# Pairs 9 to 14 of an expert loop: transposes, lists and scale rows moved behind the gate-up products, and the order of the last sums

## Chip, cores and metric

One core of one Trainium2 chip. The metric is device time in microseconds (us) of one execution; lower is better.

## What is computed

A decoder layer for 512 tokens of width 1024: an input projection, two token mixers (dilated attention and a spatial gating unit), an output projection, a first layer norm, a mixture of 32 experts and a second layer norm. The change touches only the experts and the second norm. Cut to them, the reference is:

```
gate = g_onehot[:, :, None] * e_gate[:, None, :] * p_sel[:, None, None]   # top 1 of 4 groups, top 2 of 8 experts
for g in range(N_GROUPS):
    gu = einsum('td,edf->tef', t, w_gate_up[g]);  a, b = gu[..., :256], gu[..., 256:]
    act = silu(a) * b * gate[:, g, :, None]
    y = y + einsum('tef,efd->td', act, w_down[g])
h = layer_norm(alpha * h + y, ln2_g, ln2_b)
```

## The kernel before

All 32 experts' weights (3 MB each) are streamed from HBM. Experts go in 16 pairs, p = 0 to 15 (`LAST` is 15): an expert takes up to 64 tokens, so that a pair fills 128 rows. Weights come in pieces of 1 MB, six to a pair (four of gate-up, two of down), into 20 slots in SBUF (`wc`). `wfill` puts their DMAs on the queue of the sync engine (SP), in the order of use, each as soon as its slot has been read.

One pair is:

- **Gate-up** (`gate_up`, line 900): for k = 0 to 7 the two experts' products, each over one eighth of the width, summed in one PSUM tile. Steps 0 to 3 need the first two pieces, steps 4 to 7 the other two.
- **Gating** (`gated`, lines 1080 and 1081): ScalarE (ACT) takes the silu, VectorE (DVE) multiplies, into `sa`.
- **Transposing `sa`** (`act_transposed`, lines 1088 and 1090): two transposes on TensorE (PE), a copy by ACT into `aT`.
- **Down** (`down`, line 1105): the products with the down weights; ACT copies the sums out as `y` (line 1107), DVE takes each row's mean off (1113, 1114), and GpSimd (POOL) scatters the rows to `y_dram` by an indirect DMA (1115).

Beside it, work for later pairs: `transposed` (1075, 1076) turns the next pair's gathered rows `xg` into `xTm`, in two halves of four transposes each, the first half copied by DVE, the second by ACT. `fetch(p + 3)` makes the list of tokens of the pair three further on: eight small products (873), three small DVE operations (884, 889, 879) and the gather of the rows, an indirect DMA of POOL (892). `pair_sel` (868) prepares the selection matrix for it on DVE.

PE, DVE, ACT, POOL and SP run this stage in the order in which the code issues it. In pairs 1 to 8 the down step of a pair stands inside the next pair's gate-up. From pair 9 on (`ATONCE`) it follows its own gate-up at once, so that PE stands still until `sa` and then `aT` are there. In all pairs but the last, the transposes stand between the gate-up steps k = 4, 5 and 6, and `fetch` behind k = 5.

In pair 13 (`LAST - 2`), behind k = 6, eight products (1190) spread the scale and the shift of the second norm, held in 8 rows, over 128 partitions; ACT copies the sums (1192) into the slot `ln2`, four copies of 512 columns.

**The end.** All but the last pair's rows come back from `y_dram`: eight loads (1203) bring `rb`, two summands for each of the four tiles of 128 tokens; SP issues them when the last scatter has landed. The final sum of tile i, half n, is made in PSUM (`fin[i, n]`) from three parts: `fin_x` (1151) adds the centred input of the layer, `fin_y` (1222) the last pair's rows by products with a one-hot matrix `G`, and `fin_rows` (1228, 1229) the sum of the two `rb` rows, which DVE forms for tile 0 and POOL for the others, and which PE then adds to both halves. `mb` (1260) gives the means, `nx` (1261, 1262). Then for each tile ACT squares (1236), DVE scales (1241) and writes the output (1248), and SP stores it (1249).

Before, the order on PE is: `fin_x(2, 0)`, `fin_x(2, 1)` ahead of pair 15; behind its gate-up `fin_x(0, 0)`, the transposes of `sa`, `fin_x(1, 0)`, down, `fin_y` of tiles 0 to 2 first half, `fin_x(0, 1)`, `fin_x(1, 1)`, `fin_x(3, 0)`, `mb`, `fin_y` of tiles 0 to 2 second half, both halves of tile 3, and at last `fin_rows` of all four tiles. The PSUM tiles are a ring of four (`acc`) and two rings of two (`tp`, `sc`).

Of the kernel before, what the change touches and what calls it, by code (L numbers as in the profile page):

```python
# [16 lines left out]
ALU = mybir.AluOpType  # L17
# [8 lines left out]
NT = 4  # L26
# [5 lines left out]
LAST = NPAIR - 1  # L32

ATONCE = 9
# [24 lines left out]
def layer(tc, I, out):  # L59
    nc = tc.nc  # L60
    pe, dve, act, pool_e, sp = nc.tensor, nc.vector, nc.scalar, nc.gpsimd, nc.sync
# [10 lines left out]
    def open_pool(name, side="left", space=None):  # L72
        es = ExitStack()
        kw = dict(name=name, bufs=1, side=side)
        if space != DRAM:
            kw["reuse_waits"] = "tile"
        if space is not None:
            kw["space"] = space
        p = es.enter_context(tc.tile_pool(**kw))
        stacks[name] = es  # L80
        return p
# [16 lines left out]
    def ps_acc():  # L98
        return ps_pj.tile([128, 512], F32, name="acc", bufs=4)

    def ps_t():
        return ps_tp.tile([128, 4, 128], F32, name="tp", bufs=2)

    def ps_s():
        return ps_sc.tile([128, 512], F32, name="sc", bufs=2)
# [8 lines left out]
    zeros = const.tile([128, 256], F32, name="zeros")  # L114
    x_sb = const.tile([128, NT, D], F32, name="x_sb")
    ident = const.tile([128, 128], F32, name="ident")
# [404 lines left out]
    def wfill(n):  # L521

        for src in srcs[len(wq):n]:
            t = slots[len(wq) % NSLOT]()
            if isinstance(t, list):
                for z in range(2):
                    sp.dma_start(out=t[z], in_=src[:, z * D:z * D + D])
            else:
                sp.dma_start(out=t, in_=src)
                t = [t[:, z * D:z * D + D] for z in range(2)]  # L530
            wq.append(t)
# [124 lines left out]
    op = open_pool("op")  # L656
# [214 lines left out]
    def pair_list(p, ip, a, b):  # L871
        for z in range(8):
            pe.matmul(ip[:, a:b], sels[p][:, z], vals[:, z // 2, z % 2, a:b], start=(z == 0), stop=(z == 7))
# [117 lines left out]
    xgs = [xg12[:, p] for p in range(2)]  # L991
# [71 lines left out]
    xTm = [wk.tile([128, 2, 4, 128], F32, name="xTm", bufs=2) for _ in range(2)]  # L1063
# [7 lines left out]
    def transposed(xg, xT, kk):  # L1071
        xv = xg.rearrange("s (q k) -> s k q", k=KD)
        tp = ps_t()
        for j in range(4):
            pe.transpose(out=tp[:, j], in_=xv[:, kk * 4 + j], identity=ident)  # L1075
        (act.copy if kk else dve.tensor_copy)(xT[:, kk], tp)  # L1076
# [7 lines left out]
    def act_transposed(sa):  # L1084
        av = sa.rearrange("s (q c) -> s c q", c=2)
        tp = ps_s().rearrange("p (c s) -> p c s", c=4)
        for c in range(2):
            pe.transpose(out=tp[:, c], in_=av[:, c], identity=ident)
        aT = mo.tile([128, 2, 128], F32, name="aT", bufs=1)
        act.copy(aT, tp[:, 0:2])  # L1090
        return aT

    def down(p, aT, dp=None):

        dp = dp or [ps_acc() for _ in range(2)]
        y = [wk.tile([128, D], F32R, name="y", bufs=2) for _ in range(2 if p == LAST else 1)]
        y0 = y[0].bitcast(F32)
        rs = mo.tile([128, 4], F32, name="rs", bufs=2)
        for n in range(2):
            ns = slice(n * 512, n * 512 + 512)  # L1100
            for c in range(2):
                for z in range(2):
                    zs = slice(64 * z, 64 * z + 64)
                    w = wq[6 * p + 4 + z]
                    pe.matmul(dp[n][zs], aT[:, c, zs], w[c][:, ns], start=(c == 0), stop=(c == 1))  # L1105
            if p < LAST:
                act.activation(y0[:, ns], dp[n], AF.Copy, accum_out=rs[:, n:n + 1])  # L1107
            else:
                act.activation(y[0][:, ns], dp[n], AF.Copy, accum_out=rs[:, 2 * n:2 * n + 1])
                dve.scalar_tensor_tensor(y[1][:, ns], dp[n], 1.0, y0[:, ns], op0=ALU.mult, op1=ALU.subtract,  # L1110
                                         accum_out=rs[:, 2 * n + 1:2 * n + 2])
        if p < LAST:
            dve.tensor_scalar(rs[:, 2:3], rs[:, 0:1], rs[:, 1:2], -1.0 / D, op0=ALU.add, op1=ALU.mult)  # L1113
            dve.tensor_scalar(y0, y0, rs[:, 2:3], None, op0=ALU.add)
            pool_e.indirect_dma_start(out=y_dram[:, :], out_offset=bass.IndirectOffsetOnAxis(ap=tos[p][:, 0:1], axis=0),  # L1115
                                      in_=y0, in_offset=None, bounds_check=2 * S - 1, oob_is_err=False)
        wfill(6 * p + 6 + NSLOT)
        return y, rs
# [9 lines left out]
    def fetch(p):  # L1128
        if p < NPAIR:
            ip = ps_s()  # L1130
            pair_list(p, ip, 0, 7)
            pair_tok(p, ip, 2)
            pair_out(p, ip)
            gather(p)
# [7 lines left out]
    fin = {}  # L1142
    hs = [slice(0, 512), slice(512, D)]

    def fin_x(i, n):

        if (i, n) not in fin:
            fin[i, n] = (ps_acc, ps_s, ps_t, ps_acc)[i]()
            if i == 2:
                fin[i, n] = fin[i, n].rearrange("p a b -> p (a b)")  # L1150
        pe.matmul(fin[i, n], ident, x_sb[:, i, hs[n]], start=True, stop=False)

    for p in range(1, NPAIR):
        gp = ps_acc()
        if p == 3:

            for z, n in enumerate(("ln2_g", "ln2_b")):
                pool_e.dma_start(out=zeros[4 * z:4 * z + 4], in_=I[n].rearrange("o (a d) -> (o a) d", a=4))
        if p == LAST - 2:
            ln2 = slots[16]().rearrange("p (a d) -> p a d", a=2)  # L1160
            ln2_g, ln2_b = ln2[:, 0], ln2[:, 1]
        if p == LAST:
            for n in range(2):
                fin_x(2, n)
        for k in range(KD):
            gate_up(p, [xTm[p % 2][:, kk] for kk in range(2)], k, gp)
            if k == 0:
                pair_sel(p + 3, 0, NT)
            if k == 1 and p <= ATONCE:
                aT = act_transposed(sa)  # L1170
            if k == 3:
                if p <= ATONCE:
                    down(p - 1, aT)
                wfill(6 * p + 2 + NSLOT)
            if k == 6 and LAST - 2 - NT <= p < LAST - 2:

                i = p - LAST + 2 + NT
                t = st2[:, i]
                dve.tensor_reduce(t[:, 5:6], x_sb[:, i], axis=AX.X, op=ALU.add)
                dve.tensor_scalar(t[:, 5:6], t[:, 5:6], -1.0 / D, None, op0=ALU.mult)  # L1180
                dve.tensor_scalar(x_sb[:, i], x_sb[:, i], t[:, 5:6], None, op0=ALU.add)
            if k in (4, 5) and p < LAST:
                transposed(xgs[(p + 1) % 2], xTm[(p + 1) % 2], k - 4)
            if k == 5:
                fetch(p + 3)
            if k == 6 and p == LAST - 2:
                for j in range(4):
                    b = ps_s()
                    for z in range(2):
                        pe.matmul(b[:, 256 * z:256 * z + 256], ident[0:8, 2 * j + z:2 * j + z + 1].to_broadcast([8, 128]), zeros[0:8],  # L1190
                                  start=True, stop=True)
                    act.copy(ln2[:, j // 2, hs[j % 2]], b)
        wfill(6 * p + 4 + NSLOT)
        sa = gated(gp, tgs[p][:, 1:2])
        if ATONCE <= p < LAST:
            down(p, act_transposed(sa))

    rb = []
# [8 lines left out]
    fin_x(0, 0)  # L1207
    aT = act_transposed(sa)
    fin_x(1, 0)


    o2 = [slots[z]().rearrange("p (a d) -> p a d", a=2) for z in (1, 2)]
# [7 lines left out]
    def fin_y(i, n):  # L1220
        for z in range(2):
            pe.matmul(fin[i, n], G[:, i * 128:i * 128 + 128], y[z][:, hs[n]], start=False, stop=False)

    def fin_rows(i):

        for n in range(2):
            r = rb[i][0][:, hs[n]]
            (pool_e if i else dve).tensor_tensor(r, r, rb[i][1][:, hs[n]], op=ALU.add)
            pe.matmul(fin[i, n], ident, r, start=False, stop=True)

    def ln2_scale(i):
# [19 lines left out]
    y, rs = down(LAST, aT, dp)  # L1251
    for i in range(NT - 1):
        fin_y(i, 0)
    fin_x(0, 1)
    fin_x(1, 1)
    fin_x(NT - 1, 0)

    mb = fin[NT - 1, 1] = ps_acc()
    for i in range(NT):
        pe.matmul(mb[:, 4 * i:4 * i + 4], G[:, i * 128:i * 128 + 128].bitcast(F32), rs, start=True, stop=True)  # L1260
# [1 line left out]
    dve.tensor_scalar(nx, nx, -1.0 / D, None, op0=ALU.mult)  # L1262
    for i in range(NT - 1):
        fin_y(i, 1)
    fin_y(NT - 1, 0)
    fin_x(NT - 1, 1)
    fin_y(NT - 1, 1)
    for i in range(NT):
        fin_rows(i)
    for i in range(NT):  # L1270
        ln2_scale(i)
        ln2_out(i)
# [7 lines left out]
    with tc.If(full > CAP):  # L1280
# [4 lines left out]
        with tc.For_i(0, NE, 1) as e:  # L1285
# [13 lines left out]
            for i in range(NT):  # L1299
# [6 lines left out]
                for k in range(KD):  # L1306
                    pe.matmul(gp, xT[k // 4][:, k % 4], og[k // 4][:, (k % 4) * 512:(k % 4) * 512 + 512],
                              start=(k == 0), stop=(k == KD - 1))
                aT = act_transposed(gated(gp, og_t[:, i:i + 1]))
                dp = [ps_acc() for _ in range(2)]  # L1310
                for n in range(2):
                    for c in range(2):
                        pe.matmul(dp[n], aT[:, c], od[:, c * 1024 + n * 512:c * 1024 + n * 512 + 512],
                                  start=(c == 0), stop=(c == 1))
# [38 lines left out]
```

## Time and profile before

| | us |
|---|---|
| median of 3 runs | 508.66 (508.55 to 509.71) |
| the profiled execution | 509.01 |
| its span in the profile | 507.3 |
| PE busy | 470.5 |
| DVE busy | 233.4 |
| ACT busy | 162.0 |
| POOL busy | 126.9 |

Times in the rows are counted from the start of the span. A busy time is an average over stages with different limits, so the stages around the change have to be read by themselves. A matmul record's duration is longer than the step to the next one, since they overlap; steps are read from starts, or from the chain of waits, which has them without overlap. The granted clock is given as a share of 2.4 GHz: 1.00 is 2.4 GHz and 0.50 is 1.2 GHz.

### The profile page before, as it was taken

To read this page: it belongs to the slowest core of one execution; us is meant where nothing else is said; L and a number is where in the kernel's file an instruction comes from. 1 tells how busy PE (TensorE), PEld (TensorE's weight loads), DVE (VectorE), ACT (ScalarE), POOL (GpSimd) and SP (SyncE) were. 2 spreads that over 40 slices of the span, in tenths; PEclk is the share of its full clock that TensorE was granted. 3 is DMA by queue.
4 is the path that set the end of the run, shared out by engine and by line. 5 is a ranking of instruction groups with operands and counts; after the bars stand their busy time and mean duration, and the time that the engine had idled before them with its cause. 6 is when DMAs were issued, how large, how long until landed. Compare 5 with 4: busy or idle time off the path is not lost.

```text
span 507.3 us, 6634 instructions
## 1 busy us (share of the span) xinstructions
PE 470.5 (93%) x2322; PEld 280.4 (55%) x2322; DVE 233.4 (46%) x600; ACT 162.0 (32%) x366; POOL 126.9 (25%) x194
## 2 busy tenths in 40 slices
PE   6999999999889999979999999999987988888991
PEld 5788887888767678859643333333332323323350
DVE  3586637723577548897522222222234233011056
ACT  4533536241578533123112222222221112212233
POOL 4025344000287710443111211111111010000350
PEclk9999999999999999998899999999999889979996
DMA  8744231740398549585599999999999999995624
GB/s 266 273 125 110 68 115 41 244 172 0 83 419 236 188 162 384 182 330 192 170 346 357 423 420 420 415 424 421 419 418 424 425 420 419 420 429 249 267 91 167
DMA packets 40805, 141.18 MB, mean 278 GB/s; under 512 B 10508, under 2 KB 14656, under 8 KB 28993
## 3 DMA queue, kind: packets, MB, share of 16 engines
q1 hardware_dynamic: 35808, 130.71, 67.3%
q0 software_dynamic: 4960, 10.01, 5.5%
q8 instruction: 20, 0.33, 0.3%
q14 instruction: 17, 0.13, 0.1%
HBM read 131.78 MB, written 16.25 MB: 292 GB/s over the span
## 4 chain that ended last, share of the span: by engine, by line
PE 57%; DMA 32%; DVE 7%; SPq 1%; ACT 1%; issue 1%; DVEq 0%; ACTq 0%
DMA wc<-in_w_gate_up 20%; PE acc L900 9%; PE acc L320 7%; PE acc L322 7%; PE acc L321 7%; PE acc L1105 5%; DMA wc<-in_w_down 4%; DMA wc19b<-in_w_gate_up 4%; PE acc L915 3%; DMA x_sb<-in_x 2%; PE acc L600 2%; PE tp L615 1%; PE acc L575 1%; PE acc L577 1%; PE acc L576 1%; PE tp L1075 1%
## 5 line engine op out<-in xcount | busy, mean ns | idle before, releaser
L900 PE MATMUL acc<-wc,xTm 128*64 128x512 f32 x456 | 118.0, 601 | 2.9 <-DMA wc<-in_w_gate_up 2.6
L320 PE MATMUL acc<-w_hi,xTh 128*128 128x512 f32 x160 | 65.2, 407 | 1.5 <-ACT w_hi L311 0.7
L1105 PE MATMUL acc<-wc,aT 128*64 128x512 f32 x248 | 63.7, 645 | 3.1 <-ACT aT L1090 3.1
L321 PE MATMUL acc<-w_lo,xTh 128*128 128x512 f32 x160 | 62.9, 393 | 0.5 <-DVE w_lo L312 0.5
L322 PE MATMUL acc<-w_hi,xTl 128*128 128x512 f32 x160 | 62.9, 393 | 0.0
L900 PEld LDWEIGHTS acc<-wc,xTm 128*64 128x64 f32 x456 | 31.6, 136 | 56.0 <-issue 45.3
L1115 POOL DMA_INDIRECT y_dram<-y,to x15 | 15.7, 1050 | 156.3 <-DVE xTm L1076 84.7
L1113 DVE TENSOR_SCALAR rs<-rs 128x1 f32<-128x1 f32 x15 | 3.2, 215 | 95.2 <-ACT y L1107 95.2
L312 DVE TENSOR_TENSOR w_lo<-w_raw,w_hi 128x512 fp32r<-128x512 f32 x40 | 28.1, 706 | 35.4 <-ACT w_hi L311 35.1
L311 ACT ACTIVATE w_hi<-w_raw 128x512 fp32r<-128x512 f32 x40 | 25.3, 631 | 54.2 <-PE acc L322 47.9
L1105 PEld LDWEIGHTS acc<-wc,aT 128*64 128x64 f32 x248 | 19.1, 148 | 42.1 <-issue 36.9
L1107 ACT ACTIVATE y<-acc 128x512 f32<-128x512 f32 x30 | 17.9, 597 | 61.9 <-PE acc L1105 61.9
L422 POOL TENSOR_TENSOR P<-P,st 128x128 f32<-128x128 f32 (+3 forms) x32 | 23.2, 748 | 51.1 <-DVE st L421 49.5
L320 PEld LDWEIGHTS acc<-w_hi,xTh 128*128 128x128 f32 x160 | 30.3, 189 | 8.6 <-ACT w_hi L311 1.4
L321 PEld LDWEIGHTS acc<-w_lo,xTh 128*128 128x128 f32 x160 | 30.3, 189 | 6.7 <-DVE w_lo L312 1.1
L322 PEld LDWEIGHTS acc<-w_hi,xTl 128*128 128x128 f32 x160 | 30.1, 188 | 6.7 <-DVE xTl L163 0.3
L1076 ACT COPY xTm<-tp 128x512 f32<-128x512 f32 x15 | 8.8, 585 | 63.8 <-PE tp L1075 63.8
L1075 PEld LDWEIGHTS tp<-ident,xg 128*128 128x128 f32 x120 | 15.5, 194 | 23.5 <-issue 15.4
L892 POOL DMA_INDIRECT xg<-h_dram,ti x15 | 15.8, 1050 | 43.9 <-issue 22.6
L1081 DVE SCALAR_TENSOR_TENSOR sa<-sa,tg,acc 128x256 f32<-128x256 f32 x16 | 7.6, 476 | 34.0 <-ACT sa L1080 34.0
L868 DVE TENSOR_TENSOR sel<-iota_v,slotp 128x1024 bf16<-128x1024 f32 (+2 forms) x23 | 22.5, 990 | 0.1
L1075 PE MATMUL tp<-ident,xg 128*128 128x128 f32 x120 | 21.0, 299 | 0.0
(330 smaller groups left out, 773.2 us busy)
## 6 DMA issues: line engine op xcount, KB each, us to landing
wc<-in_w_gate_up SPq DMA_DIRECT2D x61, 1024.0 KB, 20.1
wc<-in_w_down SPq DMA_DIRECT2D x31, 1024.0 KB, 20.7
w_raw<-in_w_in SPq DMA_DIRECT2D x18, 512.0 KB, 3.8
y_dram<-zeros SPq DMA_DIRECT2D x8, 512.0 KB, 7.8
wo_raw<-in_w_out SPq DMA_DIRECT2D x16, 256.0 KB, 3.6
wc<-y_dram SPq DMA_DIRECT2D x6, 512.0 KB, 7.5
x_sb<-in_x SPq DMA_DIRECT2D x8, 256.0 KB, 10.1
h_dram<-x_sb SPq DMA_DIRECT2D x4, 512.0 KB, 2.9
```

Of the source, the lines that this page charges most:

```text
L311: act.activation(wh, raw, AF.Copy)
L312: dve.tensor_tensor(wl, raw, wh.bitcast(F32), op=ALU.subtract)
L320: pe.matmul(acc[i], xh, wh, start=(k == 0), stop=False)
L321: pe.matmul(acc[i], xh, wl, start=False, stop=False)
L322: pe.matmul(acc[i], xl, wh, start=False, stop=(k == KD - 1))
L422: pool_e.tensor_tensor(P[:, 0:n], P[:, 0:n], bc(st4[:, 2:3], [128, n]), op=ALU.mult)
L868: dve.tensor_tensor(sels[p][:, 2 * a:2 * b], bc(iota_v.rearrange("p a b -> p (a b)")[:, None, :], [128, n, 128]), bc(slotp[:, p, a:b].rear ...
L892: pool_e.indirect_dma_start(out=xgs[p % 2], out_offset=None, in_=h_dram[:, :], in_offset=bass.IndirectOffsetOnAxis(ap=tis[p][:, 0:1], axis=0),
L900: pe.matmul(gp[zs], xT[k // 4][:, k % 4, zs], w[k % 4 // 2][:, k % 2 * 512:k % 2 * 512 + 512], start=(k == 0), stop=(k == KD - 1))
L1075: pe.transpose(out=tp[:, j], in_=xv[:, kk * 4 + j], identity=ident)
L1105: pe.matmul(dp[n][zs], aT[:, c, zs], w[c][:, ns], start=(c == 0), stop=(c == 1))
L1107: act.activation(y0[:, ns], dp[n], AF.Copy, accum_out=rs[:, n:n + 1])
```

## The change

For pairs 9 to 14 the two halves of `transposed` and `fetch(p + 3)` no longer stand between the gate-up steps. They follow `gated`, ahead of `act_transposed` and `down`. The eight products of the scale rows, all in pair 13 before, go to the same place: four of them, with two copies, in pair 13, and four in pair 14. At the end, `fin_x(0, 1)` and `fin_x(1, 1)` go ahead of the last down step. The sum of the two `rb` rows goes to POOL for tile 0 too. Each tile's `fin_rows` follows its `fin_y`, and all of tile 3 comes last.

```diff
-            if k in (4, 5) and p < LAST:
+            if k in (4, 5) and p < ATONCE:
                 transposed(xgs[(p + 1) % 2], xTm[(p + 1) % 2], k - 4)
-            if k == 5:
+            if k == 5 and p < ATONCE:
                 fetch(p + 3)
-            if k == 6 and p == LAST - 2:
-                for j in range(4):
-                    b = ps_s()
-                    for z in range(2):
-                        pe.matmul(b[:, 256 * z:256 * z + 256], ident[0:8, 2 * j + z:2 * j + z + 1].to_broadcast([8, 128]), zeros[0:8],
-                                  start=True, stop=True)
-                    act.copy(ln2[:, j // 2, hs[j % 2]], b)
         wfill(6 * p + 4 + NSLOT)
         sa = gated(gp, tgs[p][:, 1:2])
         if ATONCE <= p < LAST:
+            for kk in range(2):
+                transposed(xgs[(p + 1) % 2], xTm[(p + 1) % 2], kk)
+            fetch(p + 3)
+            if p >= LAST - 2:
+                a = p - LAST + 2
+                for j in range(2):
+                    b = ps_s()
+                    for z in range(2):
+                        r = 4 * a + 2 * j + z
+                        pe.matmul(b[:, 256 * z:256 * z + 256], ident[0:8, r:r + 1].to_broadcast([8, 128]), zeros[0:8],
+                                  start=True, stop=True)
+                    act.copy(ln2[:, a, hs[j]], b)
             down(p, act_transposed(sa))
...
     fin_x(1, 0)
+    fin_x(0, 1)
+    fin_x(1, 1)
...
-            (pool_e if i else dve).tensor_tensor(r, r, rb[i][1][:, hs[n]], op=ALU.add)
+            pool_e.tensor_tensor(r, r, rb[i][1][:, hs[n]], op=ALU.add)
...
     for i in range(NT - 1):
         fin_y(i, 0)
-    fin_x(0, 1)
-    fin_x(1, 1)
-    fin_x(NT - 1, 0)
-
+    fin[NT - 1, 0] = ps_acc()
     mb = fin[NT - 1, 1] = ps_acc()
...
     for i in range(NT - 1):
         fin_y(i, 1)
-    fin_y(NT - 1, 0)
-    fin_x(NT - 1, 1)
-    fin_y(NT - 1, 1)
-    for i in range(NT):
         fin_rows(i)
+    for n in range(2):
+        fin_x(NT - 1, n)
+        fin_y(NT - 1, n)
+    fin_rows(NT - 1)
     for i in range(NT):
         ln2_scale(i)
         ln2_out(i)
```

## Rows read from the trace of the kernel before

**Rows 1.** The head of the page, and of its 40 slices of the span the granted clock and the DMA share, both in tenths.

```profile
PE 470.5 (93%) x2322; PEld 280.4 (55%) x2322; DVE 233.4 (46%) x600; ACT 162.0 (32%) x366; POOL 126.9 (25%) x194
...
PEclk9999999999999999998899999999999889979996
DMA  8744231740398549585599999999999999995624
```

**Rows 2.** The chain of waits in order of time, 366 to 482 us: start, duration, what. From the weights of pair 12 to the end of the gate-up of pair 15.

```profile
393.09 22.23 DMA wc<-in_w_gate_up
...
415.38 19.85 DMA wc<-in_w_gate_up
...
436.35 0.64 PE tp L1075 x4
437.00 1.01 PE acc L900 x4
...
439.65 3.72 PE sc L1190 x16
443.37 1.06 PE acc L900 x4
...
445.41 0.71 PE sc L1088 x2
...
446.62 5.92 PE acc L1105 x16
...
459.13 1.92 PE acc L900 x8
...
462.03 0.52 PE sc L1088 x2
...
463.05 3.65 PE acc L1105 x16
...
468.62 7.02 PE acc L900 x32
```

**Rows 3.** The timeline of all engines, 388 to 464 us: start, duration, engine, line, operation, and in brackets how long the engine had stood idle and what ended that.

```profile
391.71 0.50 PE L1088 MATMUL sc<-ident,sa 128*128 128x128 f32 x2 [1.22 <-DVE sa L1081]
392.73 5.35 PE L1105 MATMUL acc<-wc,aT 128*64 128x512 f32 x16 [0.52 <-ACT aT L1090]
...
404.91 0.35 PE L873 MATMUL sc<-vals,sel 128*128 128x7 bf16 x8
...
435.28 1.07 PE L900 MATMUL acc<-wc,xTm 128*64 128x512 f32 x2 [1.43 <-DMA wc<-in_w_gate_up]
...
443.41 0.59 ACT L1192 COPY wc<-sc 128x512 f32<-128x512 f32 x1 [0.28 <-PE sc L1190]
...
462.63 0.37 ACT L1090 COPY aT<-sc 128x256 f32<-128x256 f32 x1 [1.17 <-PE sc L1088]
```

**Rows 4.** A table of stretches: the stretch and its length, busy time and instructions of PE, PE's weight loads, DVE, ACT and POOL, then the granted clock, the DMA share and GB/s.

```profile
382.00:398.00 16.00, 13.31 (x58) 4.60 (x56) 4.34 (x9) 2.03 (x5) 2.26 (x2) 0.89 1.02 425
...
414.00:429.00 15.00, 13.26 (x70) 5.08 (x68) 5.68 (x10) 2.71 (x7) 2.26 (x2) 1.00 1.02 420
...
445.00:447.00 2.00, 1.08 (x4) 0.61 (x6) 0.35 (x1) 0.37 (x1) 0.00 (x0) 0.50 1.02 430
451.00:453.00 2.00, 2.00 (x12) 0.75 (x10) 0.00 (x0) 0.44 (x2) 0.00 (x0) 0.94 1.02 430
482.00:490.00 8.00, 8.00 (x33) 5.27 (x32) 3.67 (x6) 0.32 (x2) 6.94 (x6) 1.00 0.35 141
```

**Rows 5.** DMA issues: of SP's queue the issues of the gate-up weights of pair 15 (start of the first, time to the end of the last, each 0.33 us) and of two loads of `rb` (the second of tile 0, the first of tile 1), then sizes and us from issue to landing, for issues at 444 to 448 us (the last two of those weights), at 473.3 to 474.1 (those loads) and of POOL's last scatter at 469 to 470.5.

```profile
438.57 8.21 SPq L529 DMA_DIRECT2D wc<-in_w_gate_up  x4
473.23 0.90 SPq L1203 DMA_DIRECT2D wc<-y_dram  x2
...
wc<-in_w_gate_up SPq DMA_DIRECT2D x2, 1024.0 KB, 20.7
...
wc<-y_dram SPq DMA_DIRECT2D x2, 512.0 KB, 5.6
...
y_dram<-y,to POOLq DMA_INDIRECT x1, 3.6
```

**Rows 6.** The chain of waits in order of time, 475 to 508 us.

```profile
475.64 1.05 PE acc L1151 x2
476.69 0.45 PE sc L1088 x2
477.14 0.86 PE sc L1151 x2
478.00 3.58 PE acc L1105 x16
481.59 0.66 PE acc L1222 x2
...
482.71 0.47 PE tp L1222 x2
...
485.75 0.79 PE acc L1260 x8
486.54 0.56 PE acc L1222 x2
...
489.81 0.87 PE acc L1229 x2
```

**Rows 7.** The timeline of the end, 480 to 508 us, columns as in rows 3.

```profile
480.94 2.52 POOL L1228 TENSOR_TENSOR wc<-wc 128x512 f32<-128x512 f32 x2 [7.82 <-issue]
...
485.99 3.03 POOL L1228 TENSOR_TENSOR wc<-wc 128x512 f32<-128x512 f32 x2
487.21 2.37 DVE L1228 TENSOR_TENSOR wc<-wc 128x512 f32<-128x512 f32 x2
...
493.43 1.41 DVE L1248 SCALAR_TENSOR_TENSOR wc<-acc,st,wc 128x512 f32<-128x512 f32 x2
494.80 1.88 PE L1229 MATMUL acc<-wc,ident 128*128 128x512 f32 x4
501.92 1.41 DVE L1248 SCALAR_TENSOR_TENSOR wc<-acc,st,wc 128x512 f32<-128x512 f32 x2
```

## The prediction

> **What bounds the kernel now.** I read the page first: PE is busy 93% of the span, but that mixes stages [rows 1]. The slices show a second full resource: the DMA share stands at 9 tenths from slice 20 to slice 35, some 200 us, and the clock falls in some of the same slices. So I went on to the chain of waits. Up to 435.28 us it consists of weight transfers, one behind the other, some 20 us each [rows 2]; in the table of stretches the DMA share is 1.01 to 1.02 all the way [rows 4]. In this part PE is not the bound: it catches up with the weights now and then and waits, the last time 1.43 us, until 435.28 [rows 3]. From there to the end the chain is PE, then ACT and DVE for the last tiles [rows 2, 6]. So PE time saved before 435.28 turns into longer waits for weights, and PE time saved after it counts, until a weight is late again.
>
> **Pairs 9 to 12: nothing.** Before, PE stood idle 1.22 us for `sa` in pair 10 [rows 3]. Now the eight transposes (2 x 0.64 us, [rows 2]) and the list (about 0.35 us, [rows 3]) lie there, and PE saves about the wait in each pair. The piece that ended the wait in pair 13 was issued at 415.38 and landed 19.85 us later [rows 2], in a stream that was never short of work, so the 4 x 1.2 us go into waiting. If that cover were missing, they would be a gain of up to 4.9 us; I take 0. `fetch` moves as a whole: its DVE operations now stand behind the multiplication of line 1081, which no longer waits for them; the gather stays ahead of the pair's own scatter on POOL, as before, and is issued a few us later, but its rows are asked for two pairs on; SP isn't touched, its issues stand where they stood, and the gather is not on its queue. Pairs 13 and 14 fetch nothing.
>
> **Pair 13, from 435.28 on.** Before, transposes (1.28 us), scale rows (3.72) and the way from the end of gate-up at 444.43 (443.37 + 1.06) to the start of down at 446.62 (2.19) make 7.19 us beside the gate-up products [rows 2]. After: transposes 1.28, half of the scale rows 1.86, then the transposes of `sa` and the copy. That copy now stands on ACT behind the second row copy: this starts about 0.1 us after the rows and takes 0.59, the copy to `aT` 0.37 [rows 3], with hand-overs some 1.1 us in all. Sum 4.25 us; `sa` itself (0.98 us after gate-up) is ready long before. Saved: 2.94 us.
>
> **Pair 14.** Before: 1.28 and the way from 461.05 (459.13 + 1.92) to 463.05, 2.00, so 3.28 us [rows 2]. After: the same 4.25 us as in pair 13, since half of the rows is here. Lost: 0.97 us. A gate-up step next to inserted transposes takes 1.01 us, in an undisturbed run 0.88 (7.02 / 8) [rows 2]; three or four such steps fall away: 0.4 us. At an equal clock the two pairs give 2.94 - 0.97 + 0.4 = 2.4 us.
>
> **The clock.** Down in pair 13 took 5.92 us against 3.65 in pair 14 [rows 2]: the clock was 0.50 from shortly before 445 to 451 [rows 4]. With the slower transposes of `sa` that cost 2.5 us. What went before it were the scale rows, products of 8 rows, and then the wait. In pair 10 a shorter fall followed the wait of 1.22 us: 5.35 us instead of 3.65, so 1.70 [rows 3]; in 414 to 429, in pair 12, it didn't come [rows 4]. After the change the longest wait is gone, but halves of the rows, transposes and the copy's wait now stand together, twice; and PE waits longer for weights ahead of 435. The trace shows no such order. Bounds: no fall at all (a gain of 2.5 us) and the long fall in both pairs (a loss of 2.5). I take one short fall, 1.70, the value between: of the rows with a wait, pair 10 shows it and pair 12 doesn't. That gives 0.8. Together: 3.2 us by the end of pair 15's gate-up.
>
> One rule of the Trainium skill speaks against the change. Before 435 the trace has a wait for weights of 1.43 us with no fall of the clock behind it until the scale rows [rows 3, 4]. The page "TensorE: Matmul & The Clock Gate", section "HAM oscillation — how this bites in real kernels", says that a TensorE which waits for DMA between bursts of products loses its full clock again at each burst. A PE that runs ahead of its weights would then pay at each pair; by the rule the case of two falls below is the likelier one. The row doesn't bear it out so far.
>
> **Are the weights there?** The last gate-up piece of pair 15 was issued at 446.45 (438.57 + 8.21 - 0.33) and landed 20.7 us later, at 467.2 [rows 5]; the four steps that need it take 3.5 us. Gate-up 15 can therefore not end before 470.7, while it ended at 475.64 before: at most 5.0 us can be gained up to there. 3.2 fits, and 4.9 without any fall just so.
>
> **The end.** Count from the end of gate-up 15 (475.64 before). PE's work is the same, and it is back to back in both orders, so its last product ends at 494.80 + 1.88 - 475.64 = 21.0 us in both [rows 7]. Before, the first tile's first half was complete only at 490.68 (489.81 + 0.87), 15.0 us in; ACT, DVE and the stores then needed until 503.33 for four tiles, 27.69 us in [rows 6, 7]. After: 1.05 + 0.45 + 3 x 0.86 + 3.58 (down) + 1.59 (`fin_y`) + 0.79 (`mb`) + 0.56 + 0.87 = 11.5 us to the first half of tile 0 [rows 6]. From there a first tile took 4.2 us to the end of its output (490.68 to 493.43 + 1.41) and each further one 2.83 (501.92 less 493.43, by 3) [rows 7]: tiles 0 to 2 are done at 21.3, while PE goes on. Tile 3 is complete at 21.0; from a tile's second half to the end of its output took 3.3 us (490.68 + 0.87 to 493.43 + 1.41) [rows 6, 7]. So the last output ends at 24.4 instead of 27.7: 3.3 us saved. The two `fin_x` in front of down delay it by 1.72 us, and the same 1.72 fall away behind it: no loss.
>
> The sums of the `rb` rows must keep up. Tile 0's second load was issued at 473.23 and landed about 3.2 us after the end of gate-up (473.23 + 5.6 - 475.64) [rows 5]. POOL takes 2.52 us a tile, 3.03 while DVE does the same work [rows 7]: tile 0 is ready at 5.8, asked for at 10.6; the fourth at 13.4 to 15.4, asked for at 19.3. The loads wait for the last scatter, which landed 3.6 us after issue [rows 5] and moves with pair 14. So POOL costs nothing, with 4 us of cover; a scatter or load later than that would take from the 3.3 one for one.
>
> **Sum.** 3.2 + 3.3 = 6.5 us. The profiled execution took 509.01 with a span of 507.3; it would become a span of 500.8 and a time of 502.5. That execution is 0.35 above the median, so against the median: 508.66 - 6.5 = 502.2.
>
> **Rivals.**
> - *The clock stays up* throughout: 4.9 + 3.3 = 8.2, about 500.5. For it: the longest waits are gone. Against: the scale rows remain, and the clock fell in pairs 10 and 13. 12%.
> - *The clock takes the pairs' gain back*, by the rule above or by the rows in both pairs: long falls in both, 2.4 + 2.5 - 5.0 = -0.1, only the end gains: 505.4. For it: the row ahead of the long fall was these products. 13%.
> - *The end gains nothing*, because `rb` comes over 7 us late or DVE keeps its old pace from a late start: only 3.2, 505.5. Against it: the 4 us of cover. 8%.
> - *The change does not do what it says*: pair 15's weights come 5 us later, so that the pairs only wait, and the end is held by its loads: 508.7. For it: the DMA share leaves no spare time up to slice 35 [rows 1]. Against: the landing of 467.2. 3%.
> - *Slower*: the clock falls in pairs 13, 14, 15 and at the end, and stays down longer than any row shows. Without falls the gain is 8.2 us; each us at half clock loses 0.5, so this decides from 16.4 us of it on, three stretches like that of 445 to 451. Four of them lose 4 x 2.5 us in their products and push the loads of `rb` behind their cover; I price it at 20 us of half clock, 10.0: 510.5. Against it: through 482 to 490, in one unbroken row of products, PE had 1.00 [rows 4]. 4%.
>
> **How the numbers follow.** My forecast has 60%, with 501.2 to 503.6 as its own range. The range for 8 in 10 takes in the clock's bounds, from 500.2 to 505.5. About 0.3%, 1.5 us, is what a measurement of this kernel can tell from no change. Faster by more than that are the forecast and the first three rivals, 93%; within it 3%; slower 4%.
>
> **What would show it.** Right: the chain turns from DMA to PE again at about 435; lines 1075 and 1190 behind line 1080 in pairs 13 and 14; gate-up of pair 15 ends near 472.4; the last DVE output 24.4 us after that, PE's last product 21.0 after. Wrong: a wait for gate-up weights in pair 15; a clock of 0.50 for more than about 4 us between 435 and 475; PE idle ahead of line 1229 with POOL as the releaser; or PE idle between line 1222 and line 1260.

## Result and the profile after

The changed kernel takes 502.87 us (median of 4 runs, 502.38 to 504.0), the kernel before 509.01 beside it: ratio 0.9881, 95% interval 0.986 to 0.9903. The forecast was 502.2 with a range of 500.2 to 505.5. Ratios, here and below, are of executions taken side by side and less than 1.5% above the fastest of their kernel (which leaves out one, of `early_pairs`), and they are not the quotient of the medians. The profiled execution after is the slowest of the four, 504.0 us with a span of 502.3, and it has the lowest mean granted clock of them, 0.977 against 0.981 to 0.988. The span before was 507.3, so 5.0 us are to be found between the two traces.

Line numbers behind 1190 are others in the changed kernel: 1199 and 1201 are the scale rows and their copies (1190 and 1192 before), 1209 the loads of `rb` (1203), 1230 `fin_y` (1222), 1236 and 1237 `fin_rows` (1228 and 1229), 1244 the squares (1236), 1256 the output (1248), 1266 the means (1260).

The chain of waits of the changed kernel, in order of time (start, duration, what), beside [rows 2] and [rows 6]:

```profile
436.09 6.59 PE acc L900 x14
442.68 1.09 PE tp L1075 x8
443.77 1.93 PE sc L1199 x8
...
446.21 0.38 ACT aT L1090
...
446.64 3.65 PE acc L1105 x16
450.29 6.87 PE acc L900 x32
457.16 1.09 PE tp L1075 x8
...
461.12 3.65 PE acc L1105 x16
...
466.69 7.02 PE acc L900 x32
473.70 1.06 PE acc L1151 x2
...
482.96 0.99 PE acc L1266 x8
...
484.52 1.72 PE acc L1237 x4
```

The part up to the weights of pair 13 came 0.81 us later in this execution (436.09 against 435.28 before). From there to the end of the gate-up of pair 15 (gate-up 15) it took 37.61 us (473.70 less 436.09) against 40.36 before [rows 2, 6]: 2.75 us saved. From there to the last output of DVE it takes 24.51 us (to 498.21, below) against 27.69 [rows 6, 7]: 3.18 saved. Less the 0.81, and 0.1 that is added behind the last output, these are the 5.0 us.

The timeline of the same kernel (in brackets the idle time before and what ended it) shows the two waits for weights in pair 13, then the end:

```profile
433.42 1.07 PE L900 MATMUL acc<-wc,xTm 128*64 128x512 f32 x2 [1.34 <-DMA wc<-in_w_gate_up]
...
436.09 6.59 PE L900 MATMUL acc<-wc,xTm 128*64 128x512 f32 x14 [1.60 <-DMA wc<-in_w_gate_up]
...
478.74 2.50 POOL L1236 TENSOR_TENSOR wc<-wc 128x512 f32<-128x512 f32 x2 [7.55 <-DMA wc<-y_dram]
...
487.36 2.51 POOL L1236 TENSOR_TENSOR wc<-wc 128x512 f32<-128x512 f32 x2 [0.32 <-issue]
...
496.80 1.41 DVE L1256 SCALAR_TENSOR_TENSOR wc<-acc,st,wc 128x512 f32<-128x512 f32 x2
```

Before, there was one such wait, of 1.43 us [rows 3]; PE does run further ahead of its weights. And the clock fell at another place than before: not behind the scale rows but at these waits, so that what was left of gate-up, three and a half steps, took 6.59 us. The same steps take 3.65 at full clock (in `busy_wait` below). The table of stretches (after the length: busy time of PE, its weight loads, DVE, ACT, POOL; granted clock, DMA share, GB/s):

```profile
433.00:435.00 2.00, 1.07 (x2) 0.19 (x2) 0.00 (x0) 0.00 (x0) 0.00 (x0) 1.00 0.99 414
435.00:437.00 2.00, 0.91 (x3) 0.30 (x5) 0.00 (x0) 0.00 (x0) 0.00 (x0) 0.55 1.02 424
...
441.00:443.00 2.00, 2.00 (x7) 0.62 (x5) 0.00 (x0) 0.29 (x1) 0.00 (x0) 0.74 1.00 422
```

The issue of the last gate-up piece of pair 15, and for it and for the last scatter the us from issue to landing, beside [rows 5]:

```profile
447.09 0.33 SPq L529 DMA_DIRECT2D wc<-in_w_gate_up  x1
...
wc<-in_w_gate_up SPq DMA_DIRECT2D x1, 1024.0 KB, 20.7
...
y_dram<-y,to POOLq DMA_INDIRECT x1, 6.3
```

The weights landed at 467.8, still ahead of the steps that need them (from 470.2). The scatter took 6.3 us instead of 3.6. It was issued at 467.29, while the last weights were still under way; before, it was issued some 2 us behind their landing. The other traces bear this out: 2.6 to 3.7 us in the three where it is issued behind them (`before`, `end_only`, `early_pairs`), 6.1 to 7.7 in the rest. So the loads of `rb` start as gate-up 15 ends (at 473.68), 2.8 us later against it than before, and the rows of tile 0 are there and POOL starts at 478.74, 5.0 us after it. Before, these rows landed 3.2 us after it [rows 5]. That much of the cover is gone.

### The profile page after: what moved, and what is told of

Its sections match the earlier page's. It is cut to its first block, busy times and chain, and to the rows that moved or that the text cites. A ratio compares the mean times of both kernels' runs of the same rounds, so it can differ in the third digit from the quotient of the medians.

```text
span 502.3 us, 6637 instructions
## 1 busy us (share of the span) xinstructions
PE 470.5 (94%) x2322; PEld 282.9 (56%) x2322; DVE 229.7 (46%) x598; ACT 162.3 (32%) x366; POOL 128.9 (26%) x196
## 4 chain that ended last, share of the span: by engine, by line
PE 58%; DMA 31%; DVE 5%; ACT 1%; SPq 1%; issue 1%; POOL 1%; DVEq 0%; ACTq 0%
DMA wc<-in_w_gate_up 20%; PE acc L900 9%; PE acc L320 7%; PE acc L322 7%; PE acc L321 7%; DMA wc<-in_w_down 4%; PE acc L1105 4%; DMA wc19b<-in_w_gate_up 4%; PE acc L915 3%; DMA x_sb<-in_x 2%; PE acc L600 2%; PE tp L615 2%; PE acc L575 1%; PE acc L577 1%; PE acc L576 1%; PE sc L414 1%
## 5 line engine op out<-in xcount | busy, mean ns | idle before, releaser
L900 PE MATMUL acc<-wc,xTm 128*64 128x512 f32 x456 | 122.7, 613 | 8.5 <-DMA wc<-in_w_gate_up 8.2
L900 PEld LDWEIGHTS acc<-wc,xTm 128*64 128x64 f32 x456 | 33.7, 139 | 72.4 <-issue 51.3
L1105 PE MATMUL acc<-wc,aT 128*64 128x512 f32 x248 | 58.3, 595 | 3.1 <-ACT aT L1090 3.1
L1080 ACT ACTIVATE sa<-acc 128x256 f32<-128x256 f32 x16 | 6.2, 384 | 72.7 <-PE acc L900 72.7
L420 ACT ACTIVATE P<-P,st 128x128 f32<-128x128 f32 (+3 forms) x32 | 17.9, 561 | 8.3 <-DVE st L418 8.2
```

The lines of the kernel that those rows point to most:

```text
L420: act.activation(P[:, 0:n], P[:, 0:n], AF.Exp, bias=st4[:, 0:1], scale=-1.0, accum_out=st4[:, 1:2])
L900: pe.matmul(gp[zs], xT[k // 4][:, k % 4, zs], w[k % 4 // 2][:, k % 2 * 512:k % 2 * 512 + 512], start=(k == 0), stop=(k == KD - 1))
```

## Experiments

Each line has the median, and the ratio to the kernel before on the same chip with its 95% interval. Medians before were 509.0 to 509.6.

**The two halves of the change.** `pairs_only` takes everything ahead of the line `rb = []` from the changed kernel and the rest from the kernel before; `end_only` is the reverse. Line 1235 of the one and line 1231 of the other are the products of `fin_rows`.

> The pairs changed, the end as before. My theory: two separate gains that add up, some 3 us in pairs 13 and 14 and 3.3 at the end; so here 506.0 (505.2 to 507.0), with the end of pair 15's gate-up some 2 to 3 us earlier and 27.7 us from there to the last DVE output, as before. Rival, all of the gain is the new order of the last sums: 509. Rival, all of it comes from the pairs: 503.

Measured: 506.80, 0.9934 (0.9908 to 0.996).

> The pairs as before, the end changed. My theory: 505.7 (505.2 to 506.2), gate-up of pair 15 ends near 475.6 and the last DVE output follows 24.5 us later. Rival, the end gains only because pair 15 comes earlier and the loads with it: 508 to 509. Rival, all of the gain is here: 503.

Measured: 506.74, 0.9946 (0.9922 to 0.9971). 0.66% and 0.54% make 1.20%; the whole change gives 1.19%. The halves add up, and both rivals that give all to one half fall. The chain of `pairs_only`, then that of `end_only`:

```profile
441.30 5.35 PE acc L1105 x16
...
470.06 1.06 PE acc L1151 x2
...
484.24 0.87 PE acc L1235 x2
```

```profile
446.31 5.82 PE acc L1105 x16
...
475.22 1.06 PE acc L1151 x2
...
486.03 1.72 PE acc L1231 x4
```

In `pairs_only` gate-up 15 ends at 470.06 and the first sum is complete 15.05 us later (484.24 + 0.87), as before [rows 6]. In `end_only` gate-up 15 ends where it did, and the first two sums are complete 12.5 us later (486.03 + 1.72 - 475.22), the first of them one step of 0.86 earlier. Down in pair 13 took 5.82 us there, the fall of the kernel before; in `pairs_only` the clock fell in the same place for a shorter time, and down took 5.35. The profiled execution of `pairs_only` is the fastest of its twelve (503.44), so its end of gate-up 15 is earlier than the median would have it.

**Pairs 9 to 12 alone, and without them.** `early_pairs` changes only pairs 9 to 12; `late_pairs` is the changed kernel with those left as before.

```diff
 early_pairs, against the kernel before
-            if k in (4, 5) and p < LAST:
+            if k in (4, 5) and (p < ATONCE or LAST - 2 <= p < LAST):
...
-            if k == 5:
+            if k == 5 and p < ATONCE:
...
+            if p < LAST - 2:
+                for kk in range(2):
+                    transposed(xgs[(p + 1) % 2], xTm[(p + 1) % 2], kk)
+                fetch(p + 3)
 late_pairs, against the changed kernel
-            if k in (4, 5) and p < ATONCE:
+            if k in (4, 5) and p < LAST - 2:
...
-            if k == 5 and p < ATONCE:
+            if k == 5 and p < LAST - 2:
...
-            for kk in range(2):
...
             if p >= LAST - 2:
+                for kk in range(2):
...
```

> Only pairs 9 to 12 changed; pairs 13, 14 and the end as before. My theory: these pairs are held by the weights, the time stays at 509.0 (508.5 to 509.6) while the waits for weights grow. Rival, each of the four saves its wait of 1.2 us: 504.2. Rival, a TensorE that runs ahead of its weights loses clock at the two waits of pair 13: 510.5 to 511.

Measured: 513.22, 1.0044 (1.001 to 1.0079); by the ratio 2.2 us slower than before, by the medians 4.0. The four waits gave nothing, as forecast, and something was lost, though not in every execution: five of the twelve took 508.7 to 510.1 us, as before, and seven 512.5 to 516.6. The one that was profiled is the slowest of them. Its chain from the weights of pair 13 to the end of gate-up 15, then stretches of it:

```profile
438.43 1.97 PE acc L900 x2
...
482.99 1.05 PE acc L1151 x2
```

```profile
437.00:439.00 2.00, 0.57 (x1) 0.28 (x2) 0.00 (x0) 0.00 (x0) 0.00 (x0) 0.66 0.99 414
...
445.00:447.00 2.00, 2.00 (x12) 1.40 (x8) 0.00 (x0) 0.48 (x2) 0.00 (x0) 1.00 1.00 422
...
449.00:451.00 2.00, 2.00 (x6) 0.79 (x6) 0.00 (x0) 0.82 (x2) 0.00 (x0) 0.50 0.99 418
```

The clock falls twice in pair 13: at the weights (the fall of the changed kernel) and again at the scale rows (the fall of the kernel before). This part takes 44.56 us against 40.36 before. Of the 7.6 us that its span is longer, these are 4.2; another 3.15 lie ahead of the weights of pair 13 (438.43 against 435.28), and nothing here explains them. The rival, that PE running ahead of its weights loses clock, fits the ratio roughly and this one execution; for the others it is not shown.

> As the changed kernel, but pairs 9 to 12 keep the old order. If running ahead of the weights in pairs 9 to 12 brought the fall of the clock in pair 13 at 435 to 442 us, that fall goes and the time is 500.5 to 502. If pairs 9 to 12 are neutral, 502.9. If they gave part of the gain, 504 or more.

Measured: 503.29, 0.9858 (0.9824 to 0.9893), not to be told from the whole change. So in the full change pairs 9 to 12 neither give nor take what can be measured; the faster outcome did not come. In its trace the fall at the weights of pair 13 is gone (the steps take 3.65 us), but there is one in pair 14, where down takes 5.11.

**The end.** Tile 0's sum back on DVE (`pool_e` becomes `(pool_e if i else dve)` in `fin_rows`), and the rows last:

```diff
 rows_last, against the changed kernel
     for i in range(NT - 1):
         fin_y(i, 1)
-        fin_rows(i)
...
-    fin_rows(NT - 1)
+    for i in range(NT):
+        fin_rows(i)
```

> As the changed kernel, but the sum of tile 0's two rows is DVE's again. My theory: DVE can add only behind its means, so that the first tile's first half comes about 1 us later, and the rest behind it: 503.8 (503.5 to 504.9). Rival, it makes no difference, since the new order of the products alone gives the gain: 502.9.

Measured: 506.89, 0.9938 (0.9915 to 0.9961). By the ratio three times the loss expected, by the median over four times. The timeline, and the stretch from 486 to 487 us (columns as above, the granted clock third from the end):

```profile
483.50 2.93 POOL L1236 TENSOR_TENSOR wc19g<-wc19g,wc19b 128x512 f32<-128x512 f32 x2
483.54 3.44 DVE L1236 TENSOR_TENSOR wc<-wc 128x512 f32<-128x512 f32 x2
485.36 3.65 PE L1237 MATMUL acc<-wc,ident 128*128 128x512 f32 x4 [1.79 <-DVE wc L1236]
```

```profile
486.00:487.00 1.00, 1.00 (x2) 0.00 (x0) 0.98 (x1) 0.00 (x0) 1.00 (x2) 0.50 0.00 0
```

DVE's two sums took 3.44 us, beside POOL's, where the faster of DVE's two before took 0.68. PE waits 1.79 us for the first, and its four products take 3.65 us instead of 1.72. Two things are in that: the second sum was ready only at 486.98, and the clock had fallen (0.66, 0.50, 0.50 and 0.63 in the four us from 485), so that the products start 0.85 us apart instead of 0.43. From the end of the means' products to tile 0 complete it is 6.0 us (483.03 to 489.01), in the changed kernel 2.3 (483.95 to 486.24). The difference of 3.7 us is the whole gain of the end. As an estimate from these rows, about 1.1 us of it is the clock: at full clock two products of 0.43 behind the second sum would have ended near 487.9. Three of the twelve executions took 504.0 to 504.1 us, near what was expected; whether the clock stayed up in them is not shown. On such a pair the Trainium skill, "SBUF — State Buffer", section "SBUF: two separate sides", says that a DVE operation with two inputs in SBUF and a GpSimd operation that reads SBUF exclude each other for a whole instruction. The rows agree in kind: each of DVE's sums took about as long as its own 0.68 and most of one of POOL's 1.27. It went the other way round in the kernel before, where DVE's first sum began 0.02 us ahead of one of POOL's: DVE took 0.68 and POOL 1.79.

> As the changed kernel, but the sums of the rows of all four tiles come last on TensorE, as before. My theory: completing tile after tile is what the end gains by; with it gone the time is 505.9 (505.4 to 506.4) and the last DVE output comes 27.5 us behind gate-up 15. Rival, the end gains by POOL taking tile 0 and by the two early sums ahead of down: 503 to 503.5.

Measured: 506.25, 0.9947 (0.9926 to 0.9968). The order is needed as well. Against `pairs_only` (0.9934) neither the order nor POOL gives anything alone that can be measured.

**Where the scale rows stand.** `rows_in_wait` takes them out of both fills and puts all eight into pair 13's wait for weights:

```diff
-            if p >= LAST - 2:
...
-                    act.copy(ln2[:, a, hs[j]], b)
...
+            if k == 4 and p == LAST - 2:
+                for j in range(4):
+                    b = ps_s()
+                    for z in range(2):
+                        r = 2 * j + z
+                        pe.matmul(b[:, 256 * z:256 * z + 256], ident[0:8, r:r + 1].to_broadcast([8, 128]), zeros[0:8],
+                                  start=True, stop=True)
+                    act.copy(ln2[:, j // 2, hs[j % 2]], b)
             gate_up(p, [xTm[p % 2][:, kk] for kk in range(2)], k, gp)
```

> As the changed kernel, but all eight products of the scale rows stand in pair 13 ahead of step 4, where TensorE waited 1.34 and 1.60 us for weights; none behind the gate-up. My theory: what stands between gate-up and down falls from 3.96 to about 2.05 us in pairs 13 and 14, 3.8 us less, of which the last weights of pair 15 let some 2.5 through: 500.4 (499.9 to 501.3), with gate-up of pair 15 near its weights' landing. Rival, the products of 8 rows make the clock fall wherever they stand, here ahead of a whole pair: 502.9 or more. Rival, their place costs as much as it saves: 502.9.

Measured: 501.13, 0.9848 (0.9823 to 0.9874). Gate-up 15 now waits for its weights (0.26 us), as the chain shows:

```profile
446.46 20.76 DMA wc<-in_w_gate_up
...
467.27 3.65 PE acc L900 x14
470.92 1.05 PE acc L1151 x2
```

And the clock fell, though PE had no idle moment. In stretches:

```profile
431.00:433.00 2.00, 2.00 (x10) 1.40 (x8) 0.00 (x0) 0.46 (x1) 0.25 (x1) 1.00 1.06 422
433.00:435.00 2.00, 2.00 (x9) 1.47 (x8) 0.00 (x0) 1.30 (x3) 0.00 (x0) 0.87 0.97 406
435.00:437.00 2.00, 2.00 (x6) 0.53 (x6) 0.00 (x0) 0.59 (x1) 0.00 (x0) 0.50 1.04 432
```

**What brings the fall.** `before_full`, `rows_in_wait_full` and `after_full` change one line of the kernel before, of `rows_in_wait` and of the changed kernel; `busy_wait` adds one step to the changed kernel. `after_again` is the changed kernel itself, on the chip of all of them but `after_full`.

```diff
 before_full, rows_in_wait_full, after_full: in the products of the scale rows (r is written 2 * j + z in the kernel before)
...
-    ident[0:8, r:r + 1].to_broadcast([8, 128]), zeros[0:8],
+    ident[:, r:r + 1].to_broadcast([128, 128]), zeros,
...
 busy_wait, against the changed kernel, ahead of gate_up
+            if k == 4 and p == LAST - 2:
+                wt = ps_t()
+                for z in range(20):
+                    pe.transpose(out=wt[:, z % 4], in_=ident, identity=ident)
```

> The changed kernel itself, as the measure for the three beside it on the same chip: 502.9 (502.4 to 504), as before.

Measured: 502.89, 0.9863 (0.9828 to 0.9898). Its profiled execution went another way than the first one. The timeline of pair 13, then the chain:

```profile
435.03 1.07 PE L900 MATMUL acc<-wc,xTm 128*64 128x512 f32 x2 [1.34 <-DMA wc<-in_w_gate_up]
437.88 3.65 PE L900 MATMUL acc<-wc,xTm 128*64 128x512 f32 x14 [1.78 <-DMA wc<-in_w_gate_up]
```

```profile
453.56 3.65 PE acc L900 x14
...
461.26 4.90 PE acc L1105 x16
```

The two waits for weights are there and the clock does not fall behind them. So PE is ahead of its weights once more in pair 14, where the chain turns from DMA to PE only at 453.56, and the clock falls behind the second half of the rows.

> The kernel before with one edit: the eight products of the scale rows read all 128 partitions (the others hold zeros) instead of 8; their count and columns stay. If the products of 8 rows bring the fall of the clock that follows them in pair 13, it goes, and down there takes 3.65 instead of 5.92 us: 2.5 us faster than before, 506.5. If the wait for silu brings it, nothing changes: 509.

Measured: 506.25, 0.9938 (0.9919 to 0.9958). The products of 8 rows brought the fall behind them; the waits for silu are the same (1.02 and 0.52 us), so they alone do not. With 128 rows down in pair 13 takes what it takes in pair 14, in the chain:

```profile
438.75 3.73 PE sc L1190 x16
...
445.53 3.65 PE acc L1105 x16
```

The timed executions agree: the mean granted clock of each lies between 0.974 and 0.985, in the kernel before beside them between 0.962 and 0.972.

> The kernel with all scale rows in the wait for weights of pair 13, with the same products over 128 partitions. If the 8 rows brought the fall at 434 to 441 us there, the clock stays at 1.00, and pairs 13 and 14 end some 3 us earlier; but pair 15 then waits that much longer for its last weights, so the time stays at 501.1 (500.0 to 501.5). If the fall comes from something else, it is seen again, and the time is 501.1 too. The clock in the trace tells them apart. In both cases faster than the changed kernel by 1.5 to 2.5 us.

Measured: 501.24, 0.984 (0.9808 to 0.9871). Same place, same number of products, and no fall:

```profile
431.00:433.00 2.00, 2.00 (x9) 1.35 (x8) 0.00 (x0) 0.34 (x1) 0.37 (x1) 1.00 0.98 391
433.00:435.00 2.00, 2.00 (x11) 1.44 (x9) 0.00 (x0) 1.37 (x3) 0.00 (x0) 1.00 1.02 424
435.00:437.00 2.00, 2.00 (x10) 0.89 (x10) 0.00 (x0) 0.64 (x2) 0.00 (x0) 1.00 1.01 422
```

Over its six timed executions the mean granted clock is 0.980 to 0.986, in the five of `rows_in_wait`, on another chip, 0.975 to 0.980. The time is that of `rows_in_wait`: what pair 13 gains is spent on waiting for the weights of pairs 14 and 15.

> As the changed kernel, with 20 transposes of the identity added ahead of step 4 of pair 13, whose result nobody reads; they take 2.7 us of the 4 us in which TensorE waited for weights there. If the idle wait brings the fall at 435 to 442 us, it goes, and the time falls by up to 3 us, to 500 to 501. If the clock falls anyway, or the fall in the profile was not typical of the timed runs: 502.9.

Measured: 504.72, 0.9904 (0.9872 to 0.9936), not faster than the changed kernel. The transposes took 2.40 us, and of the two waits, 2.94 us in all, 0.68 were left. The clock stayed up in pair 13 (the same steps took 3.65 us); but so it did in `after_again`, where nothing filled the waits, so that the filling kept it is not shown. Then pair 14 waited for weights, and the clock fell behind its scale rows, as in `after_again`. The timeline:

```profile
435.12 3.65 PE L900 MATMUL acc<-wc,xTm 128*64 128x512 f32 x14 [0.68 <-DMA wc<-in_w_gate_up]
...
450.97 3.65 PE L900 MATMUL acc<-wc,xTm 128*64 128x512 f32 x14 [0.30 <-DMA wc<-in_w_gate_up]
```

and stretches of it:

```profile
457.00:459.00 2.00, 1.48 (x7) 0.80 (x8) 0.00 (x0) 1.25 (x3) 0.00 (x0) 0.78 0.96 406
459.00:461.00 2.00, 2.00 (x6) 0.47 (x4) 0.00 (x0) 0.00 (x0) 0.00 (x0) 0.50 0.88 365
```

The place of the fall thus differs between executions of one kernel.

> The changed kernel with one edit: the scale rows' products read all 128 partitions instead of 8. In the traces of the changed kernel the clock fell behind the second half of the rows in pair 14 (460 to 464 us) or at the weights of pair 13 (435 to 442). If the 8 rows take part in it, the fall in pair 14 goes, and gate-up of pair 15 ends 1 to 2 us earlier, held by its weights then: 501.3 (500.8 to 502.0). If the waits alone bring it, 502.9.

Measured: 502.58, 0.9848 (0.9813 to 0.9884), which doesn't tell 501.3 from 502.9. Its profile has no fall in pair 14, but one in pair 13, at the waits, where the chain has these steps at 5.06 us:

```profile
436.80 5.06 PE acc L900 x14
```

## Why the prediction was right, and where not

**The bound** was read rightly: weights until 435, then PE. `early_pairs` shows that pairs 9 to 12 give nothing, and the chain turns to PE at 436.09. So it is in this execution. In four others the clock stayed up in pair 13 (`after_again`, `late_pairs`, `rows_last`, `busy_wait`); there the weights of pair 14 are late once more, and the chain turns only at 449.56 to 453.56. The text had allowed for a late weight, but looked for it in pair 15 only.

**Pairs 13 and 14.** The way from gate-up to down was put at 4.25 us; it is 3.96 in both (442.68 to 446.64, 457.16 to 461.12): transposes in one row take 1.09 us, not 1.28, and the copies and hand-overs 0.94, not 1.1. `sa` was ready in time, and the copy to `aT` stands behind the second row copy, as said. 3.2 us were forecast; `pairs_only` gives 0.66% or 3.4 us (its median is 2.5 below), the trace of the changed kernel 2.75. That the trace comes so near is in part luck. At equal clock its terms give 3.2 us, where 2.4 were forecast, mostly by the shorter way and by gate-up steps of 0.86 without insertions; the clock, put at 0.8 gained, lost 0.5 (2.5 saved at the old place, 2.94 lost at the new one).

**The clock.** One fall was put into the sum, and one came, but not where the text had it (behind the fill). In the profiled execution it came ahead of it, at the waits for weights in pair 13, and cost 2.94 us in products of the gate-up (6.59 less 3.65), not 1.70. One of the text's own signs of being wrong came with it, a clock of 0.50 for more than 4 us: it stood there from 436 to 442. Other executions are nearer to the text. Seven traces have half of the rows in each of pairs 13 and 14, and each shows one fall in these pairs: in two at the weights of pair 13 (2.94 and 2.78 us lost), in one behind its rows (1.70), in four behind the rows of pair 14 (1.25 to 1.46), each counted in the products of gate-up or down. The text had taken one short fall as the value between two bounds, since no row had this order of work, so this too is in part luck.

The rule that the text cites from the Trainium skill, "TensorE: Matmul & The Clock Gate", section "HAM oscillation — how this bites in real kernels", on waits for DMA is borne out by some of the traces; the page's own example has longer waits than these. Seven have both waits in pair 13, of 1.34 or 1.36 and 1.60 to 1.78 us: a fall followed in four (`after`, `after_full`, `tile0_on_dve`, `early_pairs`) and none in three (`after_again`, `pairs_only`, `rows_last`). The waits alone do not decide it. What the prediction only named, the products of 8 rows, is a cause of its own, shown by two pairs of runs.

**The end** came within 0.2 us: 24.51, forecast as 24.4 (the text's own terms, 21.0 and 3.3, make 24.3). PE's last product ended 21.3 us in, forecast 21.0. But one step was right for less than the whole reason. POOL's part was costed at nothing, against its keeping up with PE; the text left out what DVE would have cost in the new order. With the sum of tile 0 on DVE the gain is gone, by DVE's longer sums and by a fall of the clock at the wait for them. And the 4 us of cover shrank: the scatter landed in 6.3 us, so that tile 0's rows were ready at +7.5 instead of +5.8, still ahead of +10.8.

**The rivals.** The median lies below what the clock's long falls in both pairs would have given (505.4), and no trace shows both; the end gained. Slower was one of the parts, `early_pairs`, in the execution traced by falls of the clock.

Open stays how the clock decides between the places from one execution to the next, and so how much of the change's gain is clock; the executions of one kernel spread by 2 to 8 us.

**A better version.** `rows_in_wait_full` and `rows_in_wait` have the lowest medians, 501.24 and 501.13; the first ran beside the changed kernel with 502.89. Their intervals (0.9808 to 0.9871, and 0.9828 to 0.9898 for the changed kernel) overlap, so the 1.7 us are likely, not settled. In both traces the last weights of pair 15 are late, landing near 467.3.

## What to carry to other kernels

Work that one engine must do anyway belongs into a wait that another resource imposes (weights here), rather than into a short wait that it outlasts: the scale rows cost 1.9 us per pair in the wait for silu, and in the wait for weights they are off the chain. When sums are completed tile by tile to feed other engines early, check that what feeds them is not queued behind the same engine's late work: order and placement had to change together. And ahead of a stretch that waits for a stream, saved time only lengthens the wait, and may take clock from the stretch behind it.

## What the runs showed of the hardware

Eight products that read 8 partitions (3.7 us, TensorE busy without a gap) were followed by a fall to 1.2 GHz; the same eight with 128 partitions, at equal time, were not: `before_full` is 0.62% faster than the kernel before by that line alone, at a mean granted clock of 0.974 to 0.985 against 0.962 to 0.972. Four such products at a time (1.9 us) were followed by a fall in one of their two places in five traces of seven. Two waits for weights of 1.34 to 1.36 and 1.60 to 1.78 us, with half a step between them, were followed by a fall in four traces of seven. Of two sums of SBUF tiles, one of DVE and one of POOL, that met, the one that had begun later took longer: DVE 1.75 us instead of 0.68, POOL 1.79 instead of 1.28.
